# An encoder layer on one core: which projections take the seven-product form, and which engine scales the softmax

## The chip, the cores and the metric

The kernel runs on one core of one Trainium2 chip. The metric is device time in microseconds of one execution. An execution is a single launch that reads all inputs from the chip's memory and writes the output there. Five engines work beside each other, each through its instructions in their order: TensorE (PE, with its weight loads PEld), VectorE (DVE), ScalarE (ACT), GpSimd (POOL) and SyncE (SP, which only starts DMAs here). POOL starts DMAs too.

## The reference

One layer with 512 tokens, model width 2048, in float32. A projection of the normalised input gives queries, keys and values for 16 attention heads (`aq`, `ak`, `av`, 1024 columns each) and for 4 heads of gated linear attention (`gq`, `gk` 512 columns each, `gv`, `gr` 1024 each, a low-rank gate `glr`).

```python
h = rmsnorm(x, attn_norm_w)
proj = h @ w_in                                   # (512, 2048) @ (2048, 6176)
aq, ak, av, gq, gk, gv, gr, glr = split(proj)
attn = mixture_of_dilations(aq, ak, av, rel_bias_table)     # 16 heads of 64
log_a = log_sigmoid(glr @ gate_w + gate_b) / 16              # two directions
o = gla(gq * 128**-0.5, gk, gv, log_a_fwd) + reversed_gla(..., log_a_bwd)
gla_out = rmsnorm_per_head(o) * gla_norm_w * silu(gr)
x = x + concat(attn, gla_out) @ w_out
h = rmsnorm(x, ffn_norm_w)
x = x + (silu(h @ w_gate) * (h @ w_up)) @ w_down
out = rmsnorm(x, final_norm_w)
```

## The kernel before

**Numbers.** Every large product runs on TensorE in a rounded float32 format. Each operand is split into a rounded part (`hi`, a copy by ACT) and the rest (`lo`, a subtraction by DVE), and three products are summed: hi·hi, hi·lo, lo·hi.

**Two ways to make a projection.** A *job* (`run_job`) streams 512 columns of a weight in 16 *halves* (one k-tile of 128 rows each); a half costs one split (ACT L237, DVE L218) and 4 banks × 3 matmuls over 512 columns. Kind "A" gives the transposed result (lines 337 to 339), kind "B" the plain one (lines 346 to 348). A *unit* (`Feed`, and `Front` for the input projection) makes 256 columns over all 16 k-tiles with seven block products in place of eight (Strassen's scheme). It goes over four pieces; each takes sums of weight blocks (`Blocks.sums`, lines 1448 to 1450), splits (`Blocks.split`, lines 1461 and 1466), and in `Feed.products` 14 matmuls over 512 columns (L1557) and 14 over 256 (L1543). At the end `evac7` combines the seven banks (lines 1577 to 1591), adds four pieces by accumulating DMAs from POOL (lines 1602 to 1605), and `finish` scales by the row norms and stores the result in memory (L1704, L1705).

**The order.** 1. Two B jobs for `av`, under which the input is transposed and split. 2. `Front`: 14 units, namely `gr` (4), `gq` and `gk` of heads 0 and 1, `aq` and `ak` (8). 3. One A job for `gq` and `gk` of heads 2 and 3 (`evac_gqk`, stored in `gqd`). 4. Two B jobs for `gv` (`evac_gv`). 5. The jobs of `w_out`: three that take only the attention half of its rows (8 halves each, `evac_out(c, True)`), then one for column block 0 over all rows, then three more. 6. `ff`: 44 units of the feed-forward layer. 7. The product with `w_down`, and the output.

**Steps beside the jobs.** From stage 3 on, attention and the linear heads are emitted as *steps* of generators in a queue `side`. A job has a rate: `rate` steps are put between the matmuls of each half, a quarter of it after each bank (`RATES`: 3.1 in the A job and the `gv` jobs, 4.0 in the first four `w_out` jobs). `run_side` also advances a second queue, `urgent`, by one item before each step. The queue holds the low-rank gate (`low_rank`, 14 steps, 32 matmuls on lines 825 and 826), then `attention()` (142 steps), then the four linear heads (`gla`, about 120 steps). Everything is written into one program order; an engine waits only for semaphores.

**Attention.** A unit `u` is one head and 128 queries; there are 64. Its chain goes over several iterations of a loop of two steps each:
- first step of `u`: scores (PE, lines 630 and 631);
- second step of `u`: bias and row maximum (DVE L640);
- first step of `u+1`: exponential with row sum (ACT L648);
- second step of `u+2`: reciprocal (DVE L651), and for even `u` the scaling of the row by it (DVE L653);
- first step of `u+3`: for odd `u` the scaling (ACT L657);
- second step of `u+3`: four transposes (PE L662);
- then rounding (ACT L670), rest (DVE L676), product with the values (PE L686, L687), and two more to lift and add the halves (ACT L696, DVE L705).

PSUM banks come from one ring of 8, of which the running job holds 4. `read_qk` reads the next pair of heads from memory by 8 DMAs on POOL (L569), all at once, at `u % 8 == 1`; `load_qk` (ACT L592, DVE L588) splits them at `u % 8 == 4`. `scan_operands` puts two memsets and four DMAs on POOL (lines 798 to 800) at `u == 47`. `load_gla` reads `gq` and `gk` of a head on POOL (L867). In `gla`, POOL zeroes a tile (L1032) which DVE fills under a mask (L1043); the transposes of L1037 take banks that this DVE work frees. `evac_out(c, True)` adds the residual by accumulating DMAs on POOL (`load_res`, L1273). The last lines of `gla` are transposes (L1132), the gate (DVE L1135) and a split in `heads` (ACT L929, DVE L922) that makes the operands `mixh[8..15]`.

Of the kernel before, what the change touches and what calls it, by code (L numbers as in the profile page):

```python
# [15 lines left out]
F32 = mybir.dt.float32  # L16
# [7 lines left out]
P = 128  # L24
# [94 lines left out]
def layer(nc, tc, x, attn_norm_w, w_in, rel_table, gw_f, gb_f, gw_b, gb_b, gla_norm_w, w_out,  # L119
# [7 lines left out]
    with tc.manual_schedule(), \  # L127
# [432 lines left out]
        def read_qk(pr):  # L560

            f = 1 - pr % 2
            if pr < NH // 2:
                qkr[pr] = [[s2.get(F32R) for _ in range(2)] for _ in range(2)]
                for i in range(2):
                    for n in range(2):
                        src = qkd[pr // 2 * 2 + i][64 * n:64 * n + 64, f * 512:(f + 1) * 512]
                        for r in (slice(0, 64), slice(64, 128)):
                            pool.dma_start(out=qkr[pr][i][n].f[r], in_=src)  # L569

        def load_qk(pr):

# [76 lines left out]

        def att_norm(u):  # L650
            dve.reciprocal(ar[u % 4], asum[u % 4])  # L651
            if u % 2 == 0:
                dve.tensor_scalar(AT[u].t, AT[u].t, ar[u % 4], None, op0=OP.mult)  # L653

        def att_scale(u):
            if u % 2:
                act.activation(AT[u].t, AT[u].t, AF.Copy, scale=ar[u % 4])  # L657

        def att_transpose(u):
            L, t = AT[u], ps.get()  # L660
# [51 lines left out]
        def attention():  # L712


            def run(f, u, n=UNITS):
                if 0 <= u < n:
                    f(u)

            for u in range(UNITS + 7):
                h = u // 4  # L720
                if u < UNITS:
                    if u % 8 == 1:
                        read_qk(h // 2 + 1)
                    if u % 8 == 4 and h // 2 + 1 < NH // 2:
                        urgent.append(slow(load_qk(h // 2 + 1)))
                    while h // 2 not in ready:
                        run_urgent()
                run(att_scores, u)
                run(att_scale, u - 3)
                run(att_round, u - 4)  # L730
                run(att_exp, u - 1)
                if u % 2:
                    run(att_lift, (u - 7) // 2, UNITS // 2)
                mixed = None
                if "mix" in at:
                    pr = at.pop("mix")
                    f, (hi, lo) = mixf.pop(pr), s4.pair() if pr > 4 else hilo()
                    act.copy(hi.t, f.t)
                    mixed = pr, f, hi, lo
                yield  # L740
                run(att_norm, u - 2)
                run(att_transpose, u - 3)
                if u % 2 == 0:
                    run(att_av, (u - 6) // 2, UNITS // 2)
                run(att_rest, u - 4)
                run(att_max, u)
                if u % 2:
                    run(att_mix, (u - 7) // 2, UNITS // 2)
                if mixed:
                    pr, f, hi, lo = mixed  # L750
                    dve.tensor_tensor(lo.t, f.t, hi.f, op=OP.subtract)
                    put(f)
                    mixh[pr] = hi, lo
                if 34 <= u < 37:
                    load_v(1, ((0,), (1,), (2, 3))[u - 34])
                if u == 47:
                    scan_operands()
                if u == 55:
                    urgent.append(slow(gate_weights()))
                if u == UNITS - 3:  # L760
                    load_gla(0)
                yield
# [80 lines left out]
                yield  # L843
            G["gw"] = [G.pop(d) for d in range(2)]

        gqd = dr.tile([4, P, 512], F32, name="gqd")
        gfd = dr.tile([2, P, 1024], F32, name="gfd")
        gvd = dr.tile([4, P, 1024], F32, name="gvd")

        def evac_gqk(banks):  # L850
            for i in range(4):
                t = s2.get()
                if i < 2:
                    dve.scalar_tensor_tensor(t.t, banks[i].t, P ** -0.5, rb[1].t,
                                             op0=OP.mult, op1=OP.mult)
                else:
                    dve.tensor_tensor(t.t, banks[i].t, rb[1].t, op=OP.mult)
                put(banks[i])
                pool.dma_start(out=gqd[i], in_=t.t)
                put(t)  # L860

        def load_gla(h):
            if h in gq:
                return
            for i, d in enumerate((gq, gk)):
                d[h] = s2.get()
                pool.dma_start(out=d[h].t, in_=gfd[i][:, (1 - h) * 512:(2 - h) * 512] if h < 2 else gqd[2 * i + h % 2])  # L867

        def load_gv(pr):
            gv[pr] = [s4.get(F32, [P, 2, 512]) for _ in range(2)]  # L870
# [368 lines left out]
        def before_first(i):  # L1239
# [5 lines left out]
                fr.late()  # L1245

        n_front = len(jobs)
        RATES = (3.1, 4.0)
        APART = 12
        seg = [(w_in, C_GQ + 256), (w_in, C_GK + 256)]  # L1250
        job("A", [piece512(seg, None, k) for k in range(0, KT, 2)], list(range(KT)), acts_h,
            evac_gqk, rate=RATES[0], start=gstart, before=before_first, limit=3)
        for pr in range(2):
            j = job("B", [piece512(w_in, C_GV + pr * 512, k) for k in range(0, KT, 2)], list(range(KT)), acts_h,
                    evac_gv(pr), rate=RATES[0],
                    before=(lambda i: load_gates() if i == 12 else None) if pr else None)
        j.drop = lambda k: put(*hT.pop(k))

        x1 = {}
# [56 lines left out]

        def evac_out(c, part=False):
            def f(banks):
                for t in range(4):
                    if part and t // 2 in BY_ACT[c]:  # L1320
                        if t % 2 == 0:
                            res_tile(c, t // 2)
                        act.copy(x1[c][t].t, banks[t].t)
                        load_res(c, t, accum_op=OP.add)
                    else:
                        dve.tensor_tensor(x1[c][t].t, x1[c][t].t, banks[t].t, op=OP.add)
                    put(banks[t])
                if not part:
                    urgent.append(rest())

            def rest():
                yield
                for t in range(4):
                    squares(c, t, x1[c], ss2)
                    pool.dma_start(out=xd[4 * c + t], in_=x1[c][t].t)
                if c == 3:
                    dve.tensor_reduce(sum2, ss2.rearrange("p (t c) -> p t c", c=4), op=OP.add,
                                      axis=mybir.AxisListType.X)
                    rstd_of(sum2, 4, rstd2, 1.0 / D, scr)
                fs_ = {}  # L1340
                for q in (2 * c, 2 * c + 1):
                    fs_[q] = s4.get(F32, [P, 2, 512])
                    for k in range(2):
                        weighted(x1[c], 2 * q + k, W_FFN, fs_[q].t[:, k])
                    yield
                put(*x1.pop(c))
                if c == 3:
                    rb[2] = rows_of(rstd2)
                for q in (2 * c, 2 * c + 1):
                    yield from pair_operands(q, fs_.pop(q))  # L1350
            return f
# [40 lines left out]
        for c in (1, 2, 3):  # L1392
            job_out(c, 0, 8, evac_out(c, True), rate=RATES[1], start=start_out(c))
        n_in = len(jobs)
        jobs[n_front + 2].lead = lambda i: AHEAD + (i > 10) + (i > 12) + (i > 14)
        j = job_out(0, 0, KT, evac_out(0), rate=RATES[1], start=start_out(0), before=load_first)
        for j in jobs[n_front:]:
            j.fine = True
        j.drop = lambda k: drop_mix(k) if k < 8 else None
        for j in jobs[n_front + 3:]:  # L1400
            j.lead = lambda i: AHEAD + 4
        jobs[n_front + 3].lead = lambda i: AHEAD + min(4, 3 + i)
        for c in (1, 2, 3):
            j = job_out(c, 8, KT, evac_out(c), rate=1.0, before=before_out(c))
        j.drop = drop_mix
# [278 lines left out]
        class Front(Feed):  # L1684


            def __init__(self):
                self.units = [(w_in, C_GR + g * 256) for g in range(4)] + [(w_in, C_GQ), (w_in, C_GK)] + \
                    [(w_in, c + g * 256) for g in range(4) for c in (C_AQ, C_AK)]
                self.per = NP // 2  # L1690
                self.xs, self.wide, self.pre = xi, 0, {}
# [6 lines left out]
            def finish(self, u, c_, c):  # L1698
                def do():
                    r = rb[1].t[:, None, :].to_broadcast([P, 2, 512])  # L1700
                    if u == 4:
                        dve.scalar_tensor_tensor(c_.t, c_.t, P ** -0.5, r, op0=OP.mult, op1=OP.mult)
                    else:
                        dve.tensor_tensor(c_.t, c_.t, r, op=OP.mult)  # L1704
                    pool.dma_start(out=grd[u] if u < 4 else gfd[u - 4] if u < 6 else qkd[u - 6], in_=c)  # L1705
                    put(c_)

                if u == len(self.units) - 1:
# [5 lines left out]
            def run(self):  # L1714
                banks = {}
                for i, (u, q) in enumerate(self.seq):
# [14 lines left out]
                    if u == len(self.units) - 1:  # L1731
                        for p in (2 * q, 2 * q + 1):
                            put(*xi.pop(p)["slots"])
                        if q == 1:
                            read_qk(0)
                        if q == 2:
                            gla_operands()
                    done = None
# [481 lines left out]
```

## Time and profile before

| what | value |
|---|---|
| median of 3 runs | 2160.84 us (2160.28 to 2161.64) |
| the profiled execution's own time, its span | 2159.43 us, 2157.7 us |
| granted TensorE clock | 0.999 |
| PE busy | 2145.4 us (99%), 12714 matmuls |
| DVE busy | 1843.9 us (85%) |
| ACT busy | 1234.5 us (57%) |
| POOL busy | 364.0 us (17%) |
| DMA, mean | 189 GB/s |

Busy times overlap between engines. PE's busy time holds pipelined matmuls, so that its 99% says that it hardly ever stood still, not that each matmul is short. Times inside the execution are counted from the span's start.

### The profile page before, as it was taken

How to read it: one execution, taken by the hardware profiler on the slowest of the kernel's cores; microseconds unless marked ns; L12 is line 12 of the kernel's file. 1: busy time of each engine (PE TensorE's matmuls, PEld its weight loads, DVE VectorE, ACT ScalarE, POOL GpSimd, SP SyncE). 2: the span in 40 equal slices, each digit the busy share in tenths (PEclk: the TensorE clock that was granted, in tenths of full speed). 3: DMA queues.
4: the chain of work that ended last, by engine and by line, in shares of the span. 5: the costliest groups of instructions: out<-in, count | busy, mean ns of one | idle time of the engine just before them, and what ended most of it. 6: DMA issues, size and time to landing. Idle time of an engine off the chain costs nothing.

```text
span 2157.7 us, 35082 instructions
## 1 busy us (share of the span) xinstructions
PE 2145.4 (99%) x12714; PEld 1896.5 (88%) x12714; DVE 1843.9 (85%) x3187; ACT 1234.5 (57%) x2250; POOL 364.0 (17%) x501
## 2 busy tenths in 40 slices
PE   9999999999999999999999999999999999999998
PEld 7888888888888889888888888888888899999987
DVE  6699999688878788899998998998989888888885
ACT  8455555578876446455555555555555655555562
POOL 0011222211111110021112121221122220021300
PEclk9999999999999999999999999999999999999999
DMA  6377778846575873577677677776777985576982
GB/s 203 134 182 182 179 179 190 247 142 191 174 211 179 273 245 106 145 176 185 180 179 198 176 182 185 178 191 173 183 188 175 266 214 174 179 180 155 287 307 78
DMA packets 266203, 407.55 MB, mean 189 GB/s; under 512 B 19309, under 2 KB 163613, under 8 KB 266030
## 3 DMA queue, kind: packets, MB, share of 16 engines
q1 hardware_dynamic: 206238, 274.59, 40.4%
q0 software_dynamic: 59472, 130.19, 27.5%
q8 instruction: 100, 1.64, 0.3%
q14 instruction: 73, 0.60, 0.1%
q10 hardware_dynamic: 320, 0.53, 0.1%
HBM read 287.47 MB, written 66.39 MB: 164 GB/s over the span
## 4 chain that ended last, share of the span: by engine, by line
PE 58%; DVE 0%; DMA 0%; issue 0%; ACT 0%; DVEq 0%; ACTq 0%
PE ps L1557 24%; PE ps L1543 12%; PE ps L1921 5%; PE ps L1922 5%; PE ps L1920 5%; PE ps L347 1%; PE ps L346 1%; PE ps L348 1%; PE ps L2115 1%; PE ps L2117 1%; PE ps L2116 1%; DMA gd<-b 0%; DVE b L1466 0%; DVE a L2148 0%; DVE a L1577 0%
## 5 line engine op out<-in xcount | busy, mean ns | idle before, releaser
L1461 ACT CAST b<-b 128x1024 fp32r<-128x1024 f32 (+1 forms) x585 | 533.7, 944 | 387.7 <-DVE b L1466 189.8
L1466 DVE TENSOR_TENSOR b<-b,b 128x1024 fp32r<-128x1024 f32 (+1 forms) x585 | 614.2, 1084 | 32.8 <-ACT b L1461 21.2
L1557 PE MATMUL ps<-b,b 128*128 128x512 f32 x1708 | 500.6, 393 | 0.4 <-ACT b L1461 0.2
L1557 PE MATMUL ps<-a,b 128*128 128x512 f32 x1428 | 418.7, 393 | 0.1
L1557 PEld LDWEIGHTS ps<-b,b 128*128 128x128 f32 x1708 | 289.4, 188 | 32.5 <-ACT b L1461 0.7
L1543 PEld LDWEIGHTS ps<-b,b 128*128 128x128 f32 x1708 | 280.6, 190 | 40.8
L1543 PE MATMUL ps<-b,b 128*128 128x256 f32 x1708 | 307.4, 280 | 0.0
L1543 PEld LDWEIGHTS ps<-a,b 128*128 128x128 f32 x1428 | 237.0, 189 | 38.0 <-DVE b L1466 0.5
L1557 PEld LDWEIGHTS ps<-a,b 128*128 128x128 f32 x1428 | 238.5, 188 | 23.8 <-issue 0.3
L1543 PE MATMUL ps<-a,b 128*128 128x256 f32 x1428 | 256.6, 280 | 0.1
L1448 DVE TENSOR_TENSOR b<-b 128x512 f32<-128x512 f32 x268 | 183.6, 685 | 17.4 <-DMA b<-in_w_down_dram 6.9
L1920 PE MATMUL ps<-b,b 128*128 128x256 f32 x624 | 176.6, 283 | 0.0
L1921 PE MATMUL ps<-b,b 128*128 128x256 f32 x624 | 176.6, 283 | 0.0
L1922 PE MATMUL ps<-b,b 128*128 128x256 f32 x624 | 176.6, 283 | 0.0
L346 PE MATMUL ps<-b,b 128*128 128x512 f32 x332 | 133.9, 403 | 0.2 <-ACT b L455 0.2
L348 PE MATMUL ps<-b,b 128*128 128x512 f32 x332 | 130.0, 391 | 0.1
L347 PE MATMUL ps<-b,b 128*128 128x512 f32 x332 | 129.5, 390 | 0.0
L1450 DVE TENSOR_TENSOR b<-b,b 128x256 f32<-128x256 f32 x268 | 114.0, 426 | 9.2
L1449 DVE TENSOR_TENSOR b<-b,b 128x256 f32<-128x256 f32 x268 | 113.9, 425 | 9.3
L1920 PEld LDWEIGHTS ps<-b,b 128*128 128x128 f32 x624 | 119.8, 192 | 0.0
L1921 PEld LDWEIGHTS ps<-b,b 128*128 128x128 f32 x624 | 119.8, 192 | 0.0
L1922 PEld LDWEIGHTS ps<-b,b 128*128 128x128 f32 x624 | 119.8, 192 | 0.0
(308 smaller groups left out, 4040.4 us busy)
## 6 DMA issues: line engine op xcount, KB each, us to landing
b<-in_w_gate_dram SPq DMA_DIRECT2D x109, 512.0 KB, 3.9
b<-in_w_up_dram SPq DMA_DIRECT2D x88, 512.0 KB, 3.9
b<-in_w_down_dram SPq DMA_DIRECT2D x88, 512.0 KB, 5.9
b<-in_w_in_dram SPq DMA_DIRECT2D x86, 512.0 KB, 3.8
b<-a POOLq DMA_DIRECT2D x168, 256.0 KB, 4.5
b<-in_w_out_dram SPq DMA_DIRECT2D x32, 512.0 KB, 5.6
gd<-b POOLq DMA_DIRECT2D x22, 512.0 KB, 4.0
b<-gd SPq DMA_DIRECT2D x22, 512.0 KB, 8.2
```

The lines of the kernel that those rows point to most:

```text
L346: mm(o, xh.t[:, c], wh.t[:, w], start=first and not on, stop=False, skip_group_check=on)
L347: mm(o, xh.t[:, c], wl.t[:, w], start=False, stop=False, skip_group_check=on)
L348: mm(o, xl.t[:, c], wh.t[:, w], start=False, stop=last, skip_group_check=on)
L1448: dve.tensor_tensor(s_[:, :, 0:2], r[:, :, 1:3], r[:, :, 0:1].to_broadcast(shape), op=OP.add)
L1450: dve.tensor_tensor(s_[:, :, 3], s_[:, :, 2], r[:, :, 3], op=OP.add)
L1461: act.copy(o, src)
L1466: dve.tensor_tensor(o, src, h, op=OP.subtract)
L1543: mm(o, wl, xh, start=False, stop=end, skip_group_check=True)
L1557: mm(o.rearrange("p (s t) -> p s t", s=2), wh, x_, start=first and p == 0, stop=False, skip_group_check=True)
L1920: mm(o, xh[:, t], wh, start=first and h == 0, stop=False, skip_group_check=True)
L1921: mm(o, xh[:, t], wl, start=False, stop=False, skip_group_check=True)
L1922: mm(o, xl[:, t], wh, start=False, stop=last, skip_group_check=True)
```

## The change

1. The A job is gone. `gq` and `gk` of heads 2 and 3 become two more units of `Front` (16 in place of 14), stored in `gfd`, from which `load_gla` reads all four heads. The low-rank gate and attention begin with the first `gv` job.
2. The scaling of each attention row is one POOL instruction for every unit, in the second step of `u+2`; L653 on DVE and L657 on ACT are gone.
3. `read_qk` becomes a generator: two DMAs at a time, in four successive steps from `u % 8 == 0`.
4. The rate in the two `gv` jobs is 4.4 steps a half.
5. The accumulating DMAs of `evac_out(c, True)` are issued one by one through `urgent`.

```diff
@@ read_qk
                         for r in (slice(0, 64), slice(64, 128)):
                             pool.dma_start(out=qkr[pr][i][n].f[r], in_=src)
+                        yield
@@ attention
         def att_norm(u):
             dve.reciprocal(ar[u % 4], asum[u % 4])
-            if u % 2 == 0:
-                dve.tensor_scalar(AT[u].t, AT[u].t, ar[u % 4], None, op0=OP.mult)
-
-        def att_scale(u):
-            if u % 2:
-                act.activation(AT[u].t, AT[u].t, AF.Copy, scale=ar[u % 4])
+            pool.tensor_scalar(AT[u].t, AT[u].t, ar[u % 4], None, op0=OP.mult)
...
-                    if u % 8 == 1:
-                        read_qk(h // 2 + 1)
+                    if u % 8 == 0:
+                        reads = read_qk(h // 2 + 1)
+                    next(reads, None)
...
                 run(att_scores, u)
-                run(att_scale, u - 3)
                 run(att_round, u - 4)
...
                 yield
+                next(reads, None)
                 run(att_norm, u - 2)
@@ gla operands
-        gqd = dr.tile([4, P, 512], F32, name="gqd")
-        gfd = dr.tile([2, P, 1024], F32, name="gfd")
+        gfd = dr.tile([4, P, 1024], F32, name="gfd")
...
-                pool.dma_start(out=d[h].t, in_=gfd[i][:, (1 - h) * 512:(2 - h) * 512] if h < 2 else gqd[2 * i + h % 2])
+                pool.dma_start(out=d[h].t, in_=gfd[h // 2 * 2 + i][:, (1 - h % 2) * 512:(2 - h % 2) * 512])
@@ jobs
-        RATES = (3.1, 4.0)
+        RATES = (4.4, 4.0)
-        seg = [(w_in, C_GQ + 256), (w_in, C_GK + 256)]
-        job("A", [piece512(seg, None, k) for k in range(0, KT, 2)], list(range(KT)), acts_h,
-            evac_gqk, rate=RATES[0], start=gstart, before=before_first, limit=3)
         for pr in range(2):
             j = job("B", [piece512(w_in, C_GV + pr * 512, k) for k in range(0, KT, 2)], list(range(KT)), acts_h,
-                    evac_gv(pr), rate=RATES[0],
-                    before=(lambda i: load_gates() if i == 12 else None) if pr else None)
+                    evac_gv(pr), rate=RATES[0], start=None if pr else gstart, limit=3,
+                    before=(lambda i: load_gates() if i == 12 else None) if pr else before_first)
@@ evac_out
+                adds = []
...
                         act.copy(x1[c][t].t, banks[t].t)
-                        load_res(c, t, accum_op=OP.add)
+                        adds.append(t)
...
-                if not part:
-                    urgent.append(rest())
+                urgent.append(add_x(adds) if part else rest())
+
+            def add_x(ts):
+                for t in ts:
+                    yield
+                    load_res(c, t, accum_op=OP.add)
@@ Front
                 self.units = [(w_in, C_GR + g * 256) for g in range(4)] + [(w_in, C_GQ), (w_in, C_GK)] + \
+                    [(w_in, C_GQ + 256), (w_in, C_GK + 256)] + \
                     [(w_in, c + g * 256) for g in range(4) for c in (C_AQ, C_AK)]
```

More of the change, by code (lines that the diff above doesn't have):

```diff
@@ L844, in gate_weights @@
             G["gw"] = [G.pop(d) for d in range(2)]
-        gqd = dr.tile([4, P, 512], F32, name="gqd")
-        gfd = dr.tile([2, P, 1024], F32, name="gfd")
+        gfd = dr.tile([4, P, 1024], F32, name="gfd")
         gvd = dr.tile([4, P, 1024], F32, name="gvd")
[L850 to L860, printed above, removed]
         def load_gla(h):
@@ L1394, in layer @@
         n_in = len(jobs)
-        jobs[n_front + 2].lead = lambda i: AHEAD + (i > 10) + (i > 12) + (i > 14)
+        jobs[n_front + 1].lead = lambda i: AHEAD + (i > 10) + (i > 12) + (i > 14)
         j = job_out(0, 0, KT, evac_out(0), rate=RATES[1], start=start_out(0), before=load_first)
@@ L1399, in layer @@
         j.drop = lambda k: drop_mix(k) if k < 8 else None
-        for j in jobs[n_front + 3:]:
+        for j in jobs[n_front + 2:]:
             j.lead = lambda i: AHEAD + 4
-        jobs[n_front + 3].lead = lambda i: AHEAD + min(4, 3 + i)
+        jobs[n_front + 2].lead = lambda i: AHEAD + min(4, 3 + i)
         for c in (1, 2, 3):
@@ L1700, in do @@
                     r = rb[1].t[:, None, :].to_broadcast([P, 2, 512])
-                    if u == 4:
+                    if u in (4, 6):
                         dve.scalar_tensor_tensor(c_.t, c_.t, P ** -0.5, r, op0=OP.mult, op1=OP.mult)
@@ L1704, in do @@
                         dve.tensor_tensor(c_.t, c_.t, r, op=OP.mult)
-                    pool.dma_start(out=grd[u] if u < 4 else gfd[u - 4] if u < 6 else qkd[u - 6], in_=c)
+                    pool.dma_start(out=grd[u] if u < 4 else gfd[u - 4] if u < 8 else qkd[u - 8], in_=c)
                     put(c_)
@@ L1734, in run @@
                         if q == 1:
-                            read_qk(0)
+                            for _ in read_qk(0):
+                                pass
                         if q == 2:
```

## The prediction, made before the changed kernel was run

> **What bounds the kernel now.** I read the page's head first, then the busy time by stretches, then what the weight loads waited for.
>
> ```profile
> span 2157.7 us, 35082 instructions
> ...
> PE 2145.4 (99%) x12714; PEld 1896.5 (88%) x12714; DVE 1843.9 (85%) x3187; ACT 1234.5 (57%) x2250; POOL 364.0 (17%) x501
> ```
> ```profile
> core 0: us, PE busy (x) PEld busy (x) DVE busy (x) ACT busy (x) POOL busy (x), PEclk, DMA share, GB/s
> 104.40:377.70 273.30, 273.21 (x1568) 239.62 (x1568) 251.78 (x400) 144.24 (x238) 57.71 (x74) 1.00 0.74 184
> 377.70:448.40 70.70, 70.70 (x364) 57.69 (x363) 51.49 (x113) 46.53 (x100) 14.16 (x25) 1.00 0.71 202
> 448.40:525.00 76.60, 76.60 (x432) 65.56 (x431) 64.99 (x155) 59.66 (x128) 18.78 (x36) 1.00 0.60 182
> ...
> 372.00:406.00 34.00, 34.00 (x162) 26.66 (x162) 18.36 (x35) 14.59 (x32) 14.25 (x23) 1.00 1.08 298
> ```
> ```profile
> PEld ps L1037 <- DVE a L1043: 2.2, 1, 2.2
> ...
> PEld ps L662 <- DVE b L880: 0.6, 1, 0.6
> ```
>
> TensorE is busy in every stretch from end to end: the units (104 to 378 us), the A job (378 to 448) and the first `gv` job (448 to 525). Its waits are one of 2.2 us in the linear heads and crumbs like the 0.6. So the time is TensorE's work, and a change moves it in two ways only: by the matmuls that it takes out, and by waits that it makes. In the units DVE works 251.78 of 273.30 us (92%), in the `gv` job 64.99 of 76.60 (85%): full, but not the bound.
>
> **Part 1, two units for the A job.** A unit's length comes from where L1557 and L337 first run, a job's matmul from the distance of two of them.
>
> ```profile
> L1557 PE MATMUL ps<-b,b x1708: 389/393/497, 104.4 to 1695.4; 128*128 128x512 f32 x190
> ```
> ```profile
> L337 PE MATMUL ps<-b,a x52: 387/389/481, 387.0 to 448.2; 128*128 128x512 f32 x52
> ...
> L337 PE MATMUL ps<-b,b x12: 387/389/395, 377.9 to 398.3; 128*128 128x512 f32 x12
> ```
> ```profile
> 382.46 0.39 PE L337 MATMUL ps<-b,b 128*128 128x512 f32 x1
> ...
> 384.29 0.39 PE L339 MATMUL ps<-b,b 128*128 128x512 f32 x1
> ```
>
> Fourteen units take 377.9 − 104.4 = 273.5 us, 19.54 each. From the L337 at 382.46 to the L339 at 384.29 lie eight distances: 0.229 each. L337 runs 52 + 12 = 64 times and so do its two sister lines: 192 × 0.229 = 44.0 us. Two units are 39.1. **−4.9 us.** The rest of the A job's 70.7 us is the gate and attention, whose matmuls stay and move into the `gv` and `w_out` jobs. The new units bring their DVE work (about 18 us each by the first stretch) into a stretch where the other fourteen run at that density without a wait, and the A job's splits and `evac_gqk` fall away. Their POOL stores replace those to `gqd`. I cost these at nothing; the cover is the 8% that DVE has left, and if it were gone the 4.9 us would go too.
>
> **Part 2, the rate.** Low-rank gate and attention are 14 + 142 = 156 steps. Steps before the first `w_out` job were 3.1 × 15.75 × 3 = 146, now 4.4 × 15.75 × 2 = 139 (the last quarter of a job's last half gives none). So attention ends, and each linear head runs, 8 steps or two halves later. A half of the job itself is 12 × 0.229 = 2.75 us; in the first `gv` job (76.60 − 16 × 2.75) / 49.6 steps = 0.66 us of TensorE a step. A half with 4.4 steps lasts 5.65 us, a step 1.28, a unit of attention 2.57 (3.09 before).
>
> ```profile
> L653 DVE TENSOR_SCALAR a<-a,small 128x512 f32<-128x512 f32 x32 | 15.7, 489 | 1.1
> ...
> L1032 POOL MEMSET a<- 128x512 f32 x8 | 5.3, 874 | 0.7 <-ACT b L1071 0.7
> ```
> ```profile
> L657 ACT ACTIVATE a<-a,small 128x512 f32<-128x512 f32 x32 | 23.0, 720 | 3.9 <-DVE small L651 3.8
> ```
> ```profile
> L218 DVE TENSOR_TENSOR a<-b,a x71: 673/685/695, 379.3 to 1733.0; 128x512 fp32r<-128x512 f32 x71
> ```
>
> Does DVE keep up? Of its 64.99 us in the first `gv` job, 16 splits of L218 take 11.0 and half the 24.8 units' scalings 6.1; the rest is 1.93 us a unit. Now: 1.93 + 0.685 × 2/4.4 = 2.24 of 2.57, or 87%. ACT loses 0.72 on every other unit. Both keep up, but the chain of a unit has fixed lengths and a fifth less time. The one wait of this kind (0.6 at L662, after the first `gv` job) may become several: **+1.0**, between −0.6 (ACT and DVE have less to do) and +4 (0.06 us on each unit).
>
> **Part 3, the scaling on POOL.** The trace has no such operation. DVE's scaling is 0.49 us, POOL's memset of the same size 0.87: between 0.5 and, for a read and a write at the memset's pace, 1.75. I take 0.9, the row on the same engine. [...] The reciprocal comes in the second step of `u+2`, the transposes want the row in the second step of `u+3`: a unit's 2.57 us, so 0.9 is hidden, unless POOL is late. POOL runs in order, and two places make it late.
>
> The first is the start:
>
> ```profile
> 394.81 0.86 POOL L1604 DMA_DIRECT2D b<-a  x1 [11.28 <-DMA b<-a]
> 395.36 1.20 POOL L1605 DMA_DIRECT2D b<-a  x1
> 395.91 1.21 POOL L1705 DMA_DIRECT2D qkd<-b  x1
> 396.45 3.27 POOL L569 DMA_DIRECT2D a<-qkd  x5
> 401.91 0.52 POOL L569 DMA_DIRECT2D a<-qkd  x1 [2.18 <-DMA b<-a]
> 402.65 0.52 POOL L569 DMA_DIRECT2D a<-qkd  x1 [0.22 <-issue]
> 404.36 0.52 POOL L569 DMA_DIRECT2D a<-qkd  x1 [1.19 <-DMA qkd<-b]
> ```
> ```profile
> L662 PE MATMUL ps<-idn,a x256: 270/272/329, 406.9 to 605.1; 128*128 128x128 f32 x128
> ```
> ```profile
> L825 PE MATMUL ps<-b,a x16: 387/397/398, 380.6 to 393.0; 128*64 128x512 f32 x16
> ```
>
> After the last unit POOL waits 11.28 us for DMAs, then issues the reads of the second pair of heads (L569), the last of them at 404.36 because older DMAs had not landed (the DMA engines were at 1.08 of their time from 372 to 406). Before, nothing urgent stood behind these. Now the first scaling does: `norm(0)` comes in attention's sixth step, all eight reads in its first four. Counted from the job's start (377.9), POOL is free at 404.36 + 0.52 − 377.9 = 27.0, and the scaling ends at 27.9. The first transposes are the 22nd step: before, 22/3.1 = 7.1 halves (19.5) + 32 low-rank matmuls (7.3) + 8 of scores (1.8) = 28.6, and the trace has 406.9 − 377.9 = 29.0. Now 22/4.4 = 5.0 halves: 13.7 + 7.3 + 1.8 = 22.8. TensorE would wait 27.9 − 22.8 = 5.1 us. Against it: by then one weight piece less (512 KB, 1.7 us at the row's 298 GB/s) has been asked for. Ends 0 and 5.1; I take **+4.0**, since the landings and not the program set POOL's time.
>
> The second is `scan_operands`:
>
> ```profile
> 537.40 0.52 POOL L798 MEMSET a<- 32x512 f32 x1 [9.19 <-PE ps L662]
> ...
> 542.73 0.68 POOL L800 DMA_DIRECT2D a<-in_c_resets_dram  x1
> 544.01 1.06 POOL L569 DMA_DIRECT2D a<-qkd  x2 [0.60 <-issue]
> ```
>
> Its six instructions take 3.3 us of POOL at least (six of about 0.55) and 6.0 with their waits; four reads of 0.52 and a scaling follow, 6.3 in all, where the transposes leave about four steps, 5.1: **+1.2** (0 to 3). At the other pairs POOL has, over 8 units (20.6 us), 8 × 0.9 + 8 × 0.52 = 11.4 us to do: covered.
>
> **Part 4, adds one by one.**
>
> ```profile
> 632.09 4.69 POOL L1273 DMA_DIRECT2D b<-in_x_dram  x6 [21.10 <-DMA b<-in_w_gate_dram]
> 635.43 1.88 POOL L1519 DMA_DIRECT2D sd<-b  x1
> 635.97 2.34 POOL L1032 MEMSET a<- 128x512 f32 x2
> ```
>
> The wait of 2.2 us (L1037 on L1043) is this: the memsets of the first linear head stood behind six residual DMAs, and the mask behind the memsets. Now the adds are spread and the head comes two halves later: **−2.2** (−2.2 to 0). What is late next is the end:
>
> ```profile
> 745.04 1.03 PE L1132 MATMUL ps<-idn,b 128*128 128x128 f32 x8
> ...
> 748.40 1.29 DVE L922 TENSOR_TENSOR b<-a,b 128x512 fp32r<-128x512 f32 x2
> ```
>
> The last head's L1132 moves from the eleventh half of the full `w_out` job to the thirteenth. Its first operand is ready 748.40 + 0.65 − 745.04 = 4.0 us later and wanted 1.5 halves and eight transposes later, 4.1 + 1.0: **0**, up to +1.5.
>
> **Sum:** −4.9 + 1.0 + 4.0 + 1.2 − 2.2 = −0.9. The profiled execution took 2159.4, so 2158.5; the median of the runs is 1.4 above it: 2159.9. A measurement of this kernel can tell about 0.2%, 4.3 us, from no change; this is no change.
>
> **The rivals.**
>
> *R1, POOL is in time.* If the DMAs at the start land earlier than before, the +4.0 and most of the +1.2 vanish: −4.9 − 2.2 + 1.2 = −5.9, 2154.9. For it: the A job's pieces with 1024-byte rows are gone from that stretch. Against it: the 11.28 us wait belongs to the last unit, which stays.
>
> *R2, DVE pays for POOL's reads.* A unit has 0.45 splits L218, 0.5 L588 and 0.125 of the mix: 1.08 DVE operations with two inputs in SBUF, each about as long as L218's 0.685 us. If each waits half a scaling, 0.45 us, DVE needs 2.24 + 0.49 = 2.73 of 2.57: DVE becomes the bound and adds 0.16 on some 63 units, +10: 2170. It decides from 0.30 us a wait. Before, POOL had no such operation, so nothing in the trace speaks either way.
> [...]
>
> *R3, the scaling is slow.* Reads leave POOL (20.6 − 4.2) / 8 = 2.05 us a scaling. At 2.3, 0.25 × 63 = +16: 2176. Against it: the memset's 0.87.
>
> *R4, the units save nothing*, because DVE's 92% in their stretch is its limit: 2159.9 + 4.9 = 2164.8. Against it: fourteen units at 19.54 with TensorE gapless.
>
> **How the numbers follow.** Forecast 0.50 (own range 2156.5 to 2165: start 0.5 to 5.1, scan 0 to 3, lags to +4), R1 0.30, R2 0.09, R3 0.06, R4 0.05. Faster by over 0.2% (below 2156.5): R1 and the forecast's edge, 0.31. Slower (above 2165.2): R2, R3 and the forecast's other edge, 0.19. Within: 0.50. The range reaches from R1 less the 1.4 us by which the three runs differ, 2153.5, to the forecast with every added wait at its upper end (−4.9 + 4 + 5.1 + 3 + 1.5 − 2.2 = +6.5, so 2167.3) and half that scatter, 2168.0; R2 and R3, 0.15, are left out.
>
> **What would show it.** Units still 19.5 us, sixteen of them: step 1 right. One wait of TensorE at the first L662 for POOL, of 3 to 5 us: the start. None there: R1. A wait at the transposes of units 46 and 47: the scan. No wait at L1037: part 4. POOL's scaling near 0.9 us; over 2: R3. DVE's L218 and L588 longer than 0.69 us, or starting late with their inputs ready: R2. The prediction is wrong if small waits come at most units, or if TensorE waits at neither place.

## The result: slower by 0.8%, with TensorE waiting for POOL

| kernel | median of 6 runs | ratio to before |
|---|---|---|
| before | 2160.56 us (2159.33 to 2161.64) | 1 |
| changed | 2177.86 us (2175.95 to 2178.82) | 1.0079 (95%: 1.0068 to 1.0090) |

The change costs 17.3 us; the forecast was 0.7 us less than before, within a range that ended at 2168.0. The profiled execution of the changed kernel took 2175.95 us, 16.5 more than that of before. All ratios here are of fast runs alone, which leaves out one of the ten runs of experiment 2, at 2324.66 us with a granted clock of 0.85.

First the head of the profile of the changed kernel: span, and busy time, share and instructions of each engine.

```profile
span 2174.2 us, 35384 instructions
...
PE 2147.2 (99%) x12746; PEld 1896.2 (87%) x12746; DVE 1851.3 (85%) x3193; ACT 1227.0 (56%) x2236; POOL 470.9 (22%) x571
```

PE's busy time grew by 1.8 us while the span grew by 16.5: TensorE stands still for longer. POOL is the engine with more to do, 470.9 us in place of 364.0. The stretches say where: the sixteen units, then two stretches of the `gv` jobs (the first ends at 514.8 us, the second at 616) with the low-rank gate and attention beside them.

```profile
core 0: us, PE busy (x) PEld busy (x) DVE busy (x) ACT busy (x) POOL busy (x), PEclk, DMA share, GB/s
104.20:416.80 312.60, 312.52 (x1794) 274.18 (x1793) 288.08 (x458) 165.40 (x272) 65.54 (x84) 1.00 0.73 182
416.80:500.00 83.20, 74.66 (x388) 59.99 (x388) 55.73 (x130) 49.35 (x109) 50.98 (x54) 0.98 0.67 187
500.00:599.50 99.50, 92.53 (x522) 77.39 (x520) 76.88 (x189) 70.58 (x157) 71.97 (x74) 0.97 0.59 184
```

The units are as gapless as before. From 416.8 to 599.5, where attention runs, PE idles 8.5 and 7.0 us, and the granted clock, 1.00 in the stretches of before that the prediction shows, is 0.98 and 0.97. The waits of the weight loads (total us, times, longest) have one new line at their head:

```profile
PEld ps L658 <- POOL a L653: 18.8, 10, 5.0
PEld ps L631 <- DVE b L672: 1.1, 3, 0.5
...
PEld ps L1021 <- DVE a L1027: 1.0, 2, 0.8
```

L658 are the transposes (L662 before), L653 the scaling on POOL, L1021 the transposes of the linear heads (L1037 before). So 18.8 us are spent waiting for the scaled row, ten times. The scaling itself, as its source line answers (fastest, median, slowest in ns):

```profile
L653 POOL TENSOR_SCALAR a<-a,small x64: 1557/1568/1772, 443.2 to 624.0; 128x512 f32<-128x512 f32 x64
```

Three kinds of place make all but 0.5 us of the ten waits. POOL's timeline (start, duration, instruction, count, idle before) at the start, at the second pair of heads, and at `scan_operands`:

```profile
435.87 0.86 POOL L1590 DMA_DIRECT2D b<-a  x1 [10.60 <-DMA b<-a]
...
437.52 4.41 POOL L569 DMA_DIRECT2D a<-qkd  x7
442.54 0.52 POOL L569 DMA_DIRECT2D a<-qkd  x1 [0.61 <-DMA qkd<-b]
443.18 4.66 POOL L653 TENSOR_SCALAR a<-a,small 128x512 f32<-128x512 f32 x3
...
459.34 2.08 POOL L569 DMA_DIRECT2D a<-qkd  x4 [0.21 <-issue]
461.44 1.58 POOL L653 TENSOR_SCALAR a<-a,small 128x512 f32<-128x512 f32 x1
462.96 2.11 POOL L569 DMA_DIRECT2D a<-qkd  x4
465.10 4.65 POOL L653 TENSOR_SCALAR a<-a,small 128x512 f32<-128x512 f32 x3
...
572.37 0.52 POOL L795 MEMSET a<- 32x512 f32 x1
...
576.21 2.08 POOL L569 DMA_DIRECT2D a<-qkd  x4
578.31 1.58 POOL L653 TENSOR_SCALAR a<-a,small 128x512 f32<-128x512 f32 x1
```

In each, a scaling stands behind DMA issues in POOL's order. TensorE's timeline has the other side:

```profile
439.81 0.39 PE L632 MATMUL ps<-a,a 128*128 128x512 f32 x1
444.83 0.92 PE L658 MATMUL ps<-idn,a 128*128 128x128 f32 x4 [4.63 <-POOL a L653]
...
446.40 0.63 PE L348 MATMUL ps<-a,b 128*128 128x512 f32 x1
446.82 0.63 PE L631 MATMUL ps<-a,a 128*128 128x512 f32 x1
...
466.73 0.44 PE L658 MATMUL ps<-idn,a 128*128 128x128 f32 x2 [1.84 <-POOL a L653]
489.12 0.55 PE L658 MATMUL ps<-idn,a 128*128 128x128 f32 x3 [0.83 <-POOL a L653]
...
575.85 0.39 PE L348 MATMUL ps<-b,b 128*128 128x512 f32 x1
579.95 1.11 PE L658 MATMUL ps<-idn,a 128*128 128x128 f32 x4 [3.72 <-POOL a L653]
```

About 5 us at the start, about 4 at the scan, 0.8 to 1.8 at the five other pairs. (The weight loads run some 0.23 us ahead of their matmuls, L631's at 439.36 and 439.58 us, and their own waits are longer: 5.0, 4.1 and 1.3 to 2.3.) And after the long wait the matmuls follow each other at 0.42 us (446.40 to 446.82), against 0.23 elsewhere: the granted clock was lower. A window on them shows 0.58 in the third column from the right, and the stretch from 445.08 to 448.49 us is at 0.50 from end to end:

```profile
446.00:449.00 3.00, 3.00 (x11) 2.35 (x10) 1.74 (x4) 1.60 (x4) 1.84 (x2) 0.58 1.05 267
```
```profile
445.08:448.49 3.41, 3.41 (x11) 2.78 (x10) 1.27 (x2) 1.82 (x4) 2.76 (x2) 0.50 1.03 286
```

### The profile page after: what moved, and what is told of

It reads as the page before. It is cut to its first block, busy times and chain, and to the rows that moved or that the text cites. A ratio compares the mean times of both kernels' runs of the same rounds, so it can differ in the third digit from the quotient of the medians.

```text
span 2174.2 us, 35384 instructions
## 1 busy us (share of the span) xinstructions
PE 2147.2 (99%) x12746; PEld 1896.2 (87%) x12746; DVE 1851.3 (85%) x3193; ACT 1227.0 (56%) x2236; POOL 470.9 (22%) x571
## 4 chain that ended last, share of the span: by engine, by line
PE 58%; DVE 0%; DMA 0%; issue 0%; ACT 0%; DVEq 0%; ACTq 0%
PE ps L1543 24%; PE ps L1529 12%; PE ps L1910 5%; PE ps L1909 5%; PE ps L1908 5%; PE ps L346 1%; PE ps L347 1%; PE ps L348 1%; PE ps L2104 1%; PE ps L2103 1%; PE ps L2105 1%; DMA gd<-b 0%; DVE b L1452 0%; DVE a L2136 0%; DVE a L1563 0%
## 5 line engine op out<-in xcount | busy, mean ns | idle before, releaser
L1447 ACT CAST b<-b 128x1024 fp32r<-128x1024 f32 (+1 forms) x601 | 549.1, 945 | 395.3 <-DVE b L1452 200.8
L1452 DVE TENSOR_TENSOR b<-b,b 128x1024 fp32r<-128x1024 f32 (+1 forms) x601 | 630.5, 1084 | 32.3 <-ACT b L1447 20.1
L1543 PE MATMUL ps<-b,b 128*128 128x512 f32 x1760 | 517.2, 393 | 0.4 <-ACT b L1447 0.2
L1543 PE MATMUL ps<-a,b 128*128 128x512 f32 x1488 | 436.5, 393 | 0.1
L1543 PEld LDWEIGHTS ps<-b,b 128*128 128x128 f32 x1760 | 298.1, 188 | 33.2 <-ACT b L1447 0.7
L1529 PEld LDWEIGHTS ps<-b,b 128*128 128x128 f32 x1760 | 289.9, 190 | 42.4
L1529 PE MATMUL ps<-b,b 128*128 128x256 f32 x1760 | 318.0, 280 | 0.0
L1529 PEld LDWEIGHTS ps<-a,b 128*128 128x128 f32 x1488 | 246.6, 189 | 39.4 <-DVE b L1452 0.7
L1543 PEld LDWEIGHTS ps<-a,b 128*128 128x128 f32 x1488 | 248.9, 188 | 25.1 <-issue 0.3
L1529 PE MATMUL ps<-a,b 128*128 128x256 f32 x1488 | 267.5, 280 | 0.3 <-DVE b L1452 0.3
L1908 PE MATMUL ps<-b,b 128*128 128x256 f32 x624 | 176.6, 283 | 0.0
L1909 PE MATMUL ps<-b,b 128*128 128x256 f32 x624 | 176.6, 283 | 0.0
L1910 PE MATMUL ps<-b,b 128*128 128x256 f32 x624 | 176.6, 283 | 0.0
L346 PE MATMUL ps<-b,b 128*128 128x512 f32 x352 | 142.8, 406 | 0.3 <-ACT b L455 0.3
L1588 POOL DMA_DIRECT2D b<-a x58 | 50.3, 867 | 414.3 <-ACT b L1447 260.4
L348 PE MATMUL ps<-b,b 128*128 128x512 f32 x352 | 138.2, 392 | 0.2 <-DVE b L459 0.2
L347 PE MATMUL ps<-b,b 128*128 128x512 f32 x352 | 137.9, 392 | 0.0
L1435 DVE TENSOR_TENSOR b<-b,b 128x256 f32<-128x256 f32 x276 | 117.3, 425 | 9.6
L1436 DVE TENSOR_TENSOR b<-b,b 128x256 f32<-128x256 f32 x276 | 117.4, 425 | 9.5
L1908 PEld LDWEIGHTS ps<-b,b 128*128 128x128 f32 x624 | 119.8, 192 | 0.0
L1909 PEld LDWEIGHTS ps<-b,b 128*128 128x128 f32 x624 | 119.8, 192 | 0.0
```

Source lines behind the costliest of these rows:

```text
L346: mm(o, xh.t[:, c], wh.t[:, w], start=first and not on, stop=False, skip_group_check=on)
L347: mm(o, xh.t[:, c], wl.t[:, w], start=False, stop=False, skip_group_check=on)
L348: mm(o, xl.t[:, c], wh.t[:, w], start=False, stop=last, skip_group_check=on)
L1436: dve.tensor_tensor(s_[:, :, 3], s_[:, :, 2], r[:, :, 3], op=OP.add)
L1447: act.copy(o, src)
L1452: dve.tensor_tensor(o, src, h, op=OP.subtract)
```

## The experiments

Two theories stood against each other. **POOL's order**: the scaling is late because DMA issues stand ahead of it in POOL's queue. **The rate**: a unit's chain has a fifth less time at 4.4 steps a half, whoever scales. Smaller questions were the spread adds, the length of the scaling, and how the reads are spread. All lines are as in the changed kernel unless said otherwise; the ratios are to the kernel before, run on the same chip.

**1. The scaling back on DVE and ACT.**

```diff
-            pool.tensor_scalar(AT[u].t, AT[u].t, ar[u % 4], None, op0=OP.mult)
+            if u % 2 == 0:
+                dve.tensor_scalar(AT[u].t, AT[u].t, ar[u % 4], None, op0=OP.mult)
+
+        def att_scale(u):
+            if u % 2:
+                act.activation(AT[u].t, AT[u].t, AF.Copy, scale=ar[u % 4])
...
+                run(att_scale, u - 3)
```


> The changed kernel with the row scaling back on DVE (even units) and ACT (odd units); all else stays changed. Theory 1 (the loss comes from the scaling's place in POOL's queue): TensorE's waits at the transposes, 18.8 us in the weight loads' list of the changed kernel, go, and its work is 4.9 us less than before; with crumbs of about 1 us, 2155 to 2158 us. Theory 2 (at 4.4 steps a half the chain of attention is too tight whatever scales it): the waits move to other operations of attention and the time stays above 2168 us.

Measured 2162.71 us, 1.0011 (1.0001 to 1.0020). The change without its part 2 loses nearly nothing, but the 2155 to 2158 of a loss that lies in POOL's order alone was missed. The waits of this kernel:

```profile
PEld ps L663 <- ACT a L658: 6.7, 5, 3.8
...
PEld ps L631 <- DVE b L677: 2.2, 4, 0.8
```

The rows are now late on ACT. The longest wait is made by a DMA: in ACT's timeline the splits of `load_qk` (L593) wait for the reads to land, and the scaling (L658) stands behind them in ACT's order.

```profile
447.04 0.63 ACT L593 ACTIVATE a<-a 128x512 fp32r<-128x512 f32 x1 [2.27 <-DMA a<-qkd]
...
451.12 0.72 ACT L658 ACTIVATE a<-a,small 128x512 f32<-128x512 f32 x1
```

So the kernel with the tighter rate, two more units and late reads has waits of its own, without any scaling on POOL.

**2. The reads of later pairs issued by SP.** The scaling stays on POOL.

```diff
-    pool.dma_start(out=qkr[pr][i][n].f[r], in_=src)
+    (sp if pr else pool).dma_start(out=qkr[pr][i][n].f[r], in_=src)
```


> The changed kernel with the reads of the second to eighth pair of heads issued by SP; the scaling stays on POOL. Theory 1a (the scaling waits behind DMA issues): the waits at the start (5.24 us and the slowly clocked matmuls behind it) and at each later pair (1.4 to 2.5 us) go, those at the four DMAs and two memsets of the gate's operands stay (about 6 us with the slow clock): 2161 to 2166 us. Theory 1b (1.57 us a scaling is too slow by itself): little changes, over 2172 us.

Measured 2158.49 us, 0.9993 (0.9984 to 1.0003): some 19 us less than the changed kernel, and less than expected. The scaling takes as long as it did, and its waits are 3.2 us in place of 18.8:

```profile
L653 POOL TENSOR_SCALAR a<-a,small x64: 1555/1566/1574, 438.1 to 606.0; 128x512 f32<-128x512 f32 x64
```
```profile
PEld ps L658 <- POOL a L653: 3.2, 4, 2.1
```

Moving 56 DMA issues off POOL takes the whole loss away. The 19 us are more than the 15.6 us of waits that went: the half clock went too (the mean granted clock of the profiled run is 0.999, as before the change, and 0.996 in the changed kernel), some 4 us there (worked out below).

**3. The scaling on POOL alone, in the kernel before** (rate 3.1, A job, reads as before).


> The kernel before with one edit: POOL scales every row. Rate 3.1, A job and reads in one go stay. Theory 1: the eight reads in front of a scaling hold it up 4.2 us at each pair, and the transposes wait there and at the gate's operands: 2167 to 2175 us. Theory 2 (only the tighter rate makes it hurt): within 2 us of 2160.6.

Measured 2176.07 us, 1.0069 (1.0052 to 1.0085), a little above the 2167 to 2175 expected. Its waits (L657 transposes, L652 scaling, L1031 linear heads):

```profile
PEld ps L657 <- POOL a L652: 12.0, 7, 5.4
PEld ps L1031 <- DVE a L1037: 2.3, 1, 2.3
```

One part of the change, without the rate and without the units, costs 16.0 us against the 2160.03 of before beside it. That this is nearly the 17.3 of the whole change is partly chance: here the eight reads still go out all at once, and experiment 11 shows what that is worth.

**4. Experiment 1 with the residual adds all at once again.**

```diff
-                        adds.append(t)
+                        load_res(c, t, accum_op=OP.add)
...
-                urgent.append(add_x(adds) if part else rest())
+                if not part:
+                    urgent.append(rest())
```


> The kernel of e1_scale_back with the residual adds issued all at once again, as before the change. If the spreading is what took the 2.2 us wait at the linear heads' transposes away: 1 to 2.5 us slower than e1_scale_back. If the shift by two halves of a job alone did it: the same as e1_scale_back within 0.7 us.

Measured 2163.11 us, 1.0011 (1.0001 to 1.0020), the same as experiment 1. By the time, this is the second branch, that the shift alone did it. The traces say otherwise: here the linear heads wait 2.0 us for the mask, 1.0 in experiment 1's. One microsecond is less than these times can tell, so that the spreading's worth is read from the traces alone.

**5. Experiment 2, and the four DMAs of `scan_operands` on SP too.**

```diff
-                pool.dma_start(out=G["gw"][d].t[16 * d:16 * d + 16], in_=w)
+                sp.dma_start(out=G["gw"][d].t[16 * d:16 * d + 16], in_=w)
-                pool.dma_start(out=G["res"][d].t, in_=c_resets[d:d + 1].to_broadcast([P, S]))
+                sp.dma_start(out=G["res"][d].t, in_=c_resets[d:d + 1].to_broadcast([P, S]))
```


> The kernel of e2_reads_sp with the four DMAs of scan_operands issued by SP as well; its two memsets stay on POOL. If that group is what holds a scaling up there (2.1 us at one transposes' wait in e2_reads_sp), the wait falls under 0.7 us and the time by 1.5 to 2.5 us: 2156 to 2157 us. If the memsets or the chain at this unit are the cause, no change from 2158.5.

Measured 2158.17 us, 0.9989 (0.9980 to 0.9997). The waits for POOL fell to 0.6 us, but the 2156 to 2157 were not reached. The load of the bias rows (`line`) is also one of SP's. It was issued at 553.01 in experiment 2 and here, behind the added DMAs and the reads, at 567.24; DVE's bias step waits for it.

```profile
567.24 0.53 SPq L552 DMA_DIRECT2D b<-line  x1
...
573.76 0.69 DVE L641 CUSTOM_DVE_ANT_0 a<-ps,b 128x512 f32<-128x512 f32 x1 [4.08 <-DMA b<-line]
...
574.60 0.63 PE L658 MATMUL ps<-idn,a 128*128 128x128 f32 x4 [1.89 <-DVE small L652]
```

A queue was cleared by filling another: the wait moved from POOL to SP. This wait was also followed by 3.4 us at a granted clock of 0.50 (575.73 to 579.13 us); in experiment 2, with its wait of 2.1 us, the mean of the profiled run is 0.999, as before the change, and here 0.998.

**6. Experiment 3 with the reads on SP** (the edit of experiment 2 in the kernel before, with POOL's scaling).


> The kernel of e3_before_pool (before, with POOL scaling every row) with the reads of the later pairs issued by SP. Theory 1a (the 16 us of e3_before_pool are scalings behind DMA issues): 2160 to 2164 us, what is left being the gate's operands (about 4 us). If a scaling of 1.57 us is what costs: over 2170 us.

Measured 2159.45 us, 0.9997 (0.9988 to 1.0006), just under the 2160 to 2164 expected; no wait for POOL is in its list. Its scalings:

```profile
L652 POOL TENSOR_SCALAR a<-a,small x64: 1556/1566/1589, 402.8 to 599.5; 128x512 f32<-128x512 f32 x64
```

A scaling of 1.57 us makes no wait at 3.1 steps when no reads of later pairs stand in its queue. At 3.1 steps, too, the reads make the loss: some 16 us between experiments 3 and 6.

**7. Half of the row on POOL, half on DVE.**

```diff
-            pool.tensor_scalar(AT[u].t, AT[u].t, ar[u % 4], None, op0=OP.mult)
+            a, z = slice(0, 256), slice(256, 512)
+            pool.tensor_scalar(AT[u].t[:, a], AT[u].t[:, a], ar[u % 4], None, op0=OP.mult)
+            dve.tensor_scalar(AT[u].t[:, z], AT[u].t[:, z], ar[u % 4], None, op0=OP.mult)
```


> The changed kernel with POOL scaling 256 columns of each row and DVE the other 256; reads and gate operands stay on POOL. POOL's instruction falls from 1.57 us to about 0.8 if its time goes with the columns. Theory 1a: the start's wait shrinks by the 0.8 us only, the later pairs' waits of 1.4 to 2.5 us mostly go: 2164 to 2170 us. If the duration alone had made the loss: under 2160 us.

Measured 2174.90 us, 1.0069 (1.0055 to 1.0083); 2164 to 2170 was expected.

```profile
L654 POOL TENSOR_SCALAR a<-a,small x64: 913/1001/1712, 446.4 to 626.0; 128x256 f32<-128x256 f32 x64
```
```profile
PEld ps L660 <- POOL a L654: 14.3, 7, 5.8
PEld ps L631 <- DVE b L674: 5.6, 8, 1.0
```

POOL's piece is shorter by a third, its waits by a quarter, and DVE's new instruction makes waits of its own. The start even grew to 5.8: the first scaling began at 446.4 us, at 443.2 in the changed kernel. A shorter scaling behind the same queue mends little.

**8. Experiment 1 with the reads on SP**, against experiment 2: the same queues, another engine for the scaling.


> The kernel of e1_scale_back (scaling on DVE and ACT) with the reads of the later pairs issued by SP. In e1_scale_back the longest wait, 3.8 us at the first odd scaling, stood behind a split on ACT that waited for a read still behind POOL's adds. If the late reads are what is left of the loss there: 2155 to 2158 us, and the single runs lie closer together. If ACT and DVE are too tight at 4.4 steps: 2160 us or more.

Measured 2159.93 us, 0.9998 (0.9989 to 1.0007), at the edge of the second branch's 2160. The longest wait of experiment 1, 3.8 us behind a late read, is 1.8 us here.

```profile
PEld ps L663 <- ACT a L658: 4.2, 6, 1.8
PEld ps L631 <- DVE b L677: 3.4, 5, 1.1
```

At 4.4 steps a half, DVE and ACT with the scaling in them are late by 7.6 us in all. The kernel before, at 3.1 steps with the same scaling, has neither wait in its list, so that most of this is likely the price of the rate; no run varied the rate alone. With the scaling on POOL and the reads away from it, the two waits on DVE and POOL are 1.1 + 3.2. The medians are only 1.4 us apart, their intervals overlap; that POOL is the better place at this rate is read from the waits, not shown by the time.

**9. One read a step, over eight steps** (POOL, as in the changed kernel), to tell the burst from the total.

```diff
-                        yield
+                            yield
```


> The changed kernel with one read a step instead of two, over eight steps; the reads and everything else stay on POOL. POOL's total work is the same. If the loss is the burst (four reads of 0.52 us and a scaling of 1.57 us in a unit of 2.57 us, twice running): the waits at the later pairs (about 9 us in all) go for the most part and the start's 5.2 us shrinks, as fewer reads stand before the first scaling; those at the gate's operands stay: 2161 to 2167 us. If POOL's total load makes the loss: no change, 2176 to 2179 us.

Measured 2168.56 us, 1.0042 (1.0028 to 1.0055), a little above the 2161 to 2167 expected. The waits for POOL are 12.4 us, 8 times; the one at the start hardly shrank (4.7 us), those at the five other pairs fell to 4.2. The same 56 reads at half the density cost 8 to 9 us less, so the burst counts, but over four units they still need 8 × 0.52 + 4 × 1.57 = 10.4 us of 10.3: just full.

**10. Experiment 2 with `scan_operands` four units later**, away from the reads' two units.

```diff
-                if u == 47:
+                if u == 51:
```


> The kernel of e2_reads_sp with scan_operands at unit 51 instead of 47, still on POOL. With the reads on SP, POOL then has three quiet units for its memsets and DMAs. If their place beside the reads' units was the rest of the loss: the 2.1 us wait goes and 2156 to 2157 us come out. If the six instructions hold a scaling up wherever they stand: 2158 us, with the wait at the transposes four units later.

Measured **2156.36 us** (2155.17 to 2157.48), 0.9981 (0.9973 to 0.9990), as the first branch had it. It beats both kernels, the one before by 0.1 to 0.3%. Its waits, and POOL at the start:

```profile
PEld ps L1543 <- ACT b L1447: 2.1, 3, 0.8
PEld ps L658 <- POOL a L653: 2.1, 6, 0.6
```
```profile
437.15 0.86 POOL L1590 DMA_DIRECT2D b<-a  x1 [10.73 <-DMA b<-a]
...
438.92 5.37 POOL L653 TENSOR_SCALAR a<-a,small 128x512 f32<-128x512 f32 x3
```

POOL still waits 10.73 us for the last unit's DMAs, but the first scaling begins right after its three last issues and is in time. No wait for POOL is longer than 0.6 us.

**11. All eight reads at once at `u % 8 == 1`**, as in the kernel before, with the rest of the change.

```diff
-                    if u % 8 == 0:
-                        reads = read_qk(h // 2 + 1)
-                    next(reads, None)
+                    if u % 8 == 1:
+                        for _ in read_qk(h // 2 + 1):
+                            pass
...
-                next(reads, None)
```


> The changed kernel with the third part undone: all eight reads at once at the second unit of a pair, on POOL, as before the change. If the spreading over two units did neither good nor harm because the eight reads are a burst either way: 2174 to 2181 us, with one wait of 2 to 3 us a pair in place of two. If the spreading is what hurts: under 2170 us.

Measured 2192.82 us, 1.0151 (1.0135 to 1.0166), worse than the 2174 to 2181 expected.

```profile
PEld ps L658 <- POOL a L653: 28.1, 10, 5.4
```
```profile
464.07 4.17 POOL L569 DMA_DIRECT2D a<-qkd  x8
```

A block of 4.17 us per pair, and waits of 2.1 to 4.0 us at them; the mean granted clock of the profiled run is 0.992, against 0.996 in the changed kernel. Item 3 of the change, the spreading, therefore saves 15 us of what item 2 costs; the change would have been worse without it. Beside experiment 3 this shows the rate once more: with eight reads at once the scaling on POOL costs 16.0 us at 3.1 steps, and this kernel is 32 us slower than before at 4.4. The two differ by the units and the adds too.

## Why the prediction was wrong

The step that failed is the sentence on "the other pairs": 11.4 us of POOL's work in 20.6 us, "covered". It averages over the eight units of a pair. The reads stand in four successive steps, which is two units of attention: 8 × 0.52 + 2 × 0.9 = 6.0 us of work in 5.1 us by the prediction's own figures, and 7.3 us at the measured 1.57. A queue in order has to be counted over the stretch in which the work stands. Done so with its own upper bound of 1.75, the five pairs would have come to 5 × 2.6 = 13 us, and the range would have held the result. R3's threshold of 2.05 us has the same average in it.

Point by point, against the growth of the span, 16.5 us:

- **Units**: the first `gv` matmul is at 416.63, so sixteen units take 312.4 us, 19.53 each. That is 38.9 more than fourteen did, for a job of 44.0: −4.9 was right, and R4 was not what happened.
- **Rate**: +1.0 was forecast, 1.1 measured (L631 on DVE L672). The forecast had no working for the 1.0, so that its closeness is luck. That the scaling leaves DVE and ACT is needed for it: experiment 8 has 7.6 us.
- **Length of the scaling**: 0.9 was taken, with 0.5 and 1.75 as ends; it is 1.57. The nearest row, the memset at 0.87, was the wrong neighbour, and the upper end, an estimate from twice the memset's time, was nearer.
- **Start**: 5.0 us, forecast 4.0 with 5.1 as its end. POOL is free 443.06 − 416.6 = 26.5 us after the job's start (27.0 forecast). The mechanism was right, and R1 was wrong: the wait for DMAs stayed 10.60 us. That the size came out so near is in part luck: POOL was free 0.5 us earlier, and the scaling took 0.7 us longer.
- **Scan**: 4.1 us (0 to 3 was given), forecast 1.2. From 572.37 to the end of the first scaling POOL has 7.5 us (579.89), forecast 6.3: 0.5 more for the six instructions, 0.7 for the scaling. With the 5.1 of four steps that makes 2.4. The rest is in the 5.1: TensorE's last matmul before these transposes began at 575.85, so that they were due some 0.2 us later, 3.7 us and not 5.1 after 572.37.
- **Other pairs**: 18.8 − 5.0 − 4.1 = 9.7 us, forecast 0. Some 9.1 of it lies at the five pairs, the rest in two short waits elsewhere. This is the miss.
- **Half clock**: not in the prediction. After the two long waits 3.4 and 5.1 us of matmuls ran at 0.42 us in place of 0.23, at a granted clock of 0.50: about 1.6 and 2.4 us lost, an estimate from these figures.
- **Linear heads**: L1037's wait was to fall by 2.2 us; 1.0 is left, so −1.2. By the trace of experiment 4 the spreading does it, since the shift alone leaves 2.0; its time can't tell. The end of the job makes no new wait, as forecast.

The sum is −4.9 + 1.1 + 5.0 + 4.1 + 9.7 + 4.0 − 1.2 = 17.8. The matmuls themselves lose 16.2 us in the ten waits in place of the 18.8 of the loads that run ahead of them, which makes it 15.2. The two counts have the 16.5 between them, and no closer account was made.

R2, DVE held up by POOL's reads, is not the bound. POOL is busy for 61 and 72% of the two stretches of attention (50.98 of 83.20, 71.97 of 99.50), and DVE's L218, the subtraction with two inputs:

```profile
L218 DVE TENSOR_TENSOR a<-b,a x60: 671/685/948, 418.0 to 1749.5; 128x512 fp32r<-128x512 f32 x60
```

The median is the 685 of before, and the longest is 948 where it was 695. In the changed kernel 23 of DVE's subtractions with two inputs (15 of L218, 8 of `load_qk`) overlap a scaling of POOL in time, and three of these lie wholly inside one. Two of the 23, at 0.92 and 0.95 us, are longer than before; the other 21 take 0.67 to 0.69. In experiments 2 and 6, where POOL scales every row too, the longest L218 is 0.698 and 0.704 us, 0.695 in the kernel before. So DVE was not held as R2 has it. R3 comes closest in time (2176), but by another way than it states: the scaling is quicker than its threshold, and experiment 6 has it without a wait.

What stays open: the 4.9 us of the units were not run by themselves. Experiments 10 and 6 differ by units, rate, spread reads and adds, and the place of the scan, and by 3.1 us; the rest lies, as the waits of experiment 10 have it, in small waits such as the 2.1 us at L1543, whose cause was not tried. What the half clock follows from was not shown: no kernel varied that alone.

## What to carry to other kernels

On an engine that starts DMAs, arithmetic can be late, as POOL's was here: before an instruction on the critical chain goes to a queue, add up everything ahead of it over the few microseconds before its deadline, with each DMA issue at its measured length (0.52 us here) and with the waits that those issues make, and never over a mean period. When a part of a change makes a loss, look at what shares its queue first: here moving 56 DMA issues kept the scaling where it was and turned +17.3 us into −1.5, no difference that can be told, and moving one call four units later as well made it −4.1. Look at the queue that receives the work as well, as experiment 5's bias load shows.

## What the runs showed of the hardware

- POOL's scaling of a 128x512 float32 row by a number per partition takes 1.57 us, 128x256 at best 0.913: (1557 − 913) / 256 = 2.5 ns a column and about 0.27 us beside it, an estimate from these two lengths. DVE's same instruction took 0.489 in the kernel before.
- POOL's scaling and DVE's subtractions with two inputs ran side by side: of the 23 that overlapped in the changed kernel, 21 kept their 0.67 to 0.69 us.
- A wait of TensorE can cost more than its length. In the changed kernel the granted clock fell to 0.50 at 445.08 us, just after the weight loads' wait of 5.0 us, for 3.41 us (the row stands with the result), and at 578.20, within the one of 4.1 us, for 6.82. It was 1.00 after the one of 2.28 us that ended at 466.73 (third column from the right):

```profile
466.73 0.42 PEld L658 LDWEIGHTS ps<-idn,a 128*128 128x128 f32 x4 [2.28 <-POOL a L653]
```
```profile
466.73:472.00 5.27, 5.27 (x31) 4.61 (x32) 3.06 (x7) 3.00 (x8) 3.33 (x3) 1.00 0.49 136
574.78:578.19 3.41, 1.45 (x8) 0.91 (x6) 1.79 (x5) 1.58 (x4) 3.12 (x7) 1.00 0.60 161
578.20:585.02 6.82, 5.07 (x17) 4.19 (x17) 2.29 (x5) 1.30 (x3) 6.76 (x8) 0.50 0.53 156
```

  The length of the loads' wait alone did not decide it: experiment 5's was of 2.28 us as well, and 0.50 followed. In experiment 11 the matmuls stood still for 3.41 − 1.73 = 1.68 us of one stretch and 3.40 − 1.90 = 1.50 of the next, and the clock was 1.00 in both. What decides was not shown. The lines (experiment 5 first):

```profile
574.57 0.42 PEld L658 LDWEIGHTS ps<-idn,a 128*128 128x128 f32 x4 [2.28 <-issue]
```
```profile
572.31:575.72 3.41, 1.52 (x9) 1.06 (x8) 1.96 (x6) 1.12 (x3) 1.03 (x1) 1.00 1.06 413
575.73:579.13 3.40, 3.40 (x12) 2.75 (x11) 3.21 (x7) 3.38 (x9) 1.00 (x2) 0.50 1.03 397
```
```profile
567.95:571.36 3.41, 1.73 (x10) 1.17 (x8) 2.57 (x9) 1.80 (x4) 3.41 (x8) 1.00 0.85 259
571.37:574.77 3.40, 1.90 (x14) 1.83 (x15) 0.59 (x1) 1.21 (x3) 3.40 (x3) 1.00 0.43 122
```
